# A scan beside attention: its pairs' ranks set 80 apart instead of 50

## The chip, the cores and the metric

The kernel runs on one core of a Trainium2 chip. A core has five engines that each run their own queue of instructions in order: TensorE (PE; matrix products, its weight loads are counted apart as PEld), VectorE (DVE), ScalarE (ACT), GpSimd (POOL) and SyncE (SP, which here only issues transfers). The time is device microseconds of one execution. Before the change, three runs gave a median of 3282.74 us (3273.26 to 3292.82).

## The reference

The kernel computes one block of a transformer over 1024 tokens (a grid of 16 by 64) and 256 context tokens, width 1024. A modulated layer norm is projected to three kinds of columns. Those of the first kind go to a neighbourhood attention with 8 heads of 64, those of the second to a two-directional RWKV scan with 8 heads of 64, those of the third are gates. The two results are merged and go through a router to a mixture of 16 experts.

```
row_block(i):                       # attention: one row of the grid
    kb, vb = window of 8 rows x 16 columns around each query
    s = [qi.kb * scale + bias, qi.k_ctx * scale];  p = softmax(s)
    return p_loc.vb + p_ctx.v_ctx
...
scan, per direction and head:       # state S (64 x 64), token by token
    S = decay(w) * S + rank-one updates from (kk, a) and (k, v);  y = r.S
...
y = group_norm(y_forward + y_backward) + bonus * v;  y = y * g      # readout
merged = gate_a * (na.w_pa) + gate_b * (y.w_pr);  x += merged.w_o
router -> top tokens per expert -> gated MLP of width 2816 -> x
```

## The kernel before, in words

Products of full precision are split into a high and a low part, so that one product becomes two or three on PE.

The stages are written one after another, but they are not run so. A scheduler takes the instructions of all engines and writes each engine's queue: of what is ready it puts the one with the lowest priority number first. The number counts up as instructions are written, and a `with low_priority(tc,n)` adds n to it for what is written inside. Each engine then runs its queue in order and waits at each instruction for what it needs.

- *Projection* (L264, `pp`) with the features of the scan and a small inversion (L298 to L326). It fills the transfers that the scan later loads.
- *Scan*, `rwkv_chain`. There are 20 pairs (j, n), and a pair is two steps, one for each direction d. A step loads five operands on SP (cAV, cX, cWT, cBT, cAU, L550 to L554, double-buffered), makes eight groups of eight 64x64 products (L541, through `mm`), reads `RU` on ACT into R (L559) and U (L566), and updates the state S on DVE (L568, L569). The trace has two records for each product, so a pair leaves 256 records of L541. The next step of the same direction needs S.
- *Attention*, `attention`, in two halves. The first takes head pairs 0 and 1, the second head pairs 2 and 3. For every head pair `run` first prepares Q and K: loads qz on ACT's queue (L633), a shuffle on DVE (L635), the rotation on POOL (L636 to L638), then KH, KL and Q (L642, L643, L648, L649). Then follow eight blocks. A block has scores `sc` and `sl` (L594 to L597), the bias and row maximum on DVE (L598, L599; each leaves two records per head, so four of L598 a block), the exponential on ACT (L602), scaling on DVE (L605), transposes `apt` (L612) and copies `pT` (L614, L616), and the products with V (L619).
- *Readout* (L677 to L702): eight tiles that add both directions' y, normalise and transpose them. L702 is a tile's last instruction. Readout and the second half of the attention need PSUM that the scan holds, so they begin when it ends.
- *Modulation* (L119, L120) for the merge.
- *Branches*: the attention result times w_pa and the scan's times w_pr, L716, 384 products; the one with w_pr comes first. Its weights are loaded by SP into `mwr` (L708), in memory that the fourth head pair's preparation frees (`done` in `run`). Then L759 merges, and the router and the experts follow.

The second head pair of each half follows the first as its blocks run out, so a preparation stands between the blocks of two head pairs.

Of the kernel before, what the change touches and what calls it, by code (L numbers as in the profile page):

```python
# [151 lines left out]
def mixer(octx, tc, i, G, keep, mc, dbg=None):  # L152
# [32 lines left out]
    with ExitStack() as c1:  # L185
# [300 lines left out]
        with ExitStack() as cw:  # L486
            wk=pool(cw,"wk",2,side="right"); pR=pool(cw,"wkR",1,space=PS,side="right")
            rwkv_chain(wk,pR,tc,i,G)
# [30 lines left out]
def tblock(j,d):  # L519

    return 0 if j==0 else (j if d==0 else 5-j)

def rwkv_chain(p,pR,tc,i,G):


    nc=tc.nc; vD=G["vD"]; yD=G["yD"]
    S=[p.tile([128,4,64],F32,name=f"S{d}",bufs=1) for d in range(2)]
    DL=[p.tile([128,4,20],F32,name=f"DLs{d}",bufs=1) for d in range(2)]
    for d in range(2): nc.sync.dma_start(DL[d],G["DLD"][d].rearrange("a p c -> p a c"))
    H=[slice(0,64),slice(64,128)]  # L530
    VS={}
    for b in (0,1,4,2,3):
        VS[b]=p.tile([128,4,4,64],F32,name=f"V{b}",bufs=1)
        for h,hh in zip(H,range(2)):
            nc.sync.dma_start(VS[b][h],vD[b*256:b*256+256,hh].rearrange("(c p) a f -> p c a f",p=64))
    def mm(o,l,r,first=None,stop=False):

        for ct in range(4):
            for hh,h in enumerate(H):
                b=first is not None and len(first)<2  # L540
                z=nc.tensor.matmul(o[h,ct],l[h,ct],r[h,ct],start=b,stop=stop,skip_group_check=True)  # L541
                if b: first.append(z)
                elif first: tc.add_manual_dep(z.ins,first[hh].ins.name,mybir.DependencyInfo(mybir.DependencyClass.NoSync,mybir.DependencyReason.DATA),reason="order")
    def step(j,n,d):
        main=j>0; tb=tblock(j,d); c=n if d==0 else 3-n; cc=tb*4+c
        first=(j==0 and n==0); M=128 if main else 64
        X,AV=[p.tile([128,4,128],F32,name=f"{z}{d}") for z in ("cX","cAV")]
        AU,WT,U=[p.tile([128,4,64],F32,name=f"{z}{d}") for z in ("cAU","cWT","U")]; V=VS[tb][:,c]
        BT=p.tile([128,2,4,64],F32,name=f"cBT{d}")
        nc.sync.dma_start(AV[:,:,:M],G["AVD"][d][cc][:,:,:M])  # L550
        nc.sync.dma_start(X[:,:,:M],G["XD"][d][cc][:,:,:M])
        nc.sync.dma_start(WT,G["WD"][d][cc].rearrange("h s a t -> (h s) a t"))
        nc.sync.dma_start(BT,G["BTD"][d][cc])
        if main: nc.sync.dma_start(AU,G["AUD"][d][cc])  # L554
        RU=pR.tile([128,2,4,64],F32,name=f"RU{d}"); YS=pR.tile([128,2,4,64],F32,name=f"YS{d}")
        mm(RU[:,0],AV[:,:,0:64],V,[],first)
        if not first: mm(RU[:,0],X[:,:,0:64],S[d],stop=True)
        R=p.tile([128,4,64],F32,name=f"R{d}",bufs=1)
        nc.scalar.activation(R,RU[:,0],AF.Copy,scale=-1.0)  # L559
        f=[]  # L560
        mm(YS[:,1],BT[:,1],V,f)
        if main:
            mm(YS[:,0],AV[:,:,64:128],V,f)
            mm(YS[:,0],X[:,:,64:128],S[d])
        mm(RU[:,1],WT,R,stop=True)
        nc.scalar.copy(U,RU[:,1])  # L566
        mm(YS[:,1],BT[:,0],U,stop=True)
        if not first: nc.vector.tensor_add(S[d],S[d],YS[:,1])  # L568
        nc.vector.tensor_tensor(S[d],YS[:,1] if first else S[d],DL[d][:,:,cc:cc+1].to_broadcast([128,4,64]),op=ALU.mult)  # L569
        if main:  # L570
            mm(YS[:,0],AU,U,stop=True)
            Y=p.tile([128,4,64],F32,name="Y",bufs=3)
            nc.scalar.copy(Y,YS[:,0])
            for h,hh in zip(H,range(2)): nc.sync.dma_start(yD[d][(cc-4)*64:(cc-3)*64,hh],Y[h])
    for j in range(5):
        for n in range(4):
            with low_priority(tc,2920-96*(4*j+n)):
                for d in range(2): step(j,n,d)

def attention(p,pr,tc,i,G):  # L580
# [527 lines left out]
```

## Time and profile before

| what | value |
|---|---|
| median of 3 runs | 3282.74 us |
| profiled execution | 3280.36 us |
| its span | 3278.5 us |
| mean granted TensorE clock | 0.947 |
| PE busy | 3018.6 us (92%) |
| DVE busy | 2291.9 us (70%) |
| ACT busy | 1732.9 us (53%) |
| POOL busy | 592.8 us (18%) |

The profile is of one execution. Busy time is the time in which an engine runs an instruction; PE's products are pipelined, so a busy PE is not PE at its peak. The granted clock is what the chip's throttle allowed, 1.00 being 2.4 GHz. The scan, the first half of the attention, the readouts and the start of the second half lie between about 890 and 1393 us of the span; the experts take the second half of it.

### The profile page before, as it was taken

Reading aid. Unit: us, or ns where it says so; the run is one execution under the profiler, and the core shown is the slowest. Engines: PE = TensorE matmul, PEld = TensorE weight load, DVE = VectorE, ACT = ScalarE, POOL = GpSimd, SP = SyncE. Lnnn points to the kernel's source line nnn. Section 1 sums busy time; section 2 is a strip of 40 time slices with the busy share of each in tenths; the row PEclk is TensorE's granted clock in tenths of the full one; section 3 lists DMA queues with packets and bytes.
Section 4 is the critical chain, followed back from the end, with each engine's and each line's share of the span. In section 5 each row is a group of like instructions: output and inputs, shape, how many; then the busy total and the mean of one; then the engine's idle time right before and its main releaser. Section 6 shows DMA issues by size and latency. Waiting matters only on the chain.

```text
span 3278.5 us, 51242 instructions
## 1 busy us (share of the span) xinstructions
PE 3018.6 (92%) x19868; PEld 2390.2 (73%) x19868; DVE 2291.9 (70%) x3049; ACT 1732.9 (53%) x2006; POOL 592.8 (18%) x429
## 2 busy tenths in 40 slices
PE   7998999997779988799979999999999999999996
PEld 4777777775568763477748888788888888888884
DVE  5246356454233448757878988888988889889887
ACT  5343433333122333432337777777777777777775
POOL 2243333333030027303000000110001111000004
PEclk8999989997789999799979999999999999999998
DMA  5345554554757546345389999999999999999985
GB/s 202 80 124 134 136 129 106 136 149 111 188 164 213 160 146 209 95 128 175 138 314 372 370 368 371 359 379 382 364 365 357 359 373 374 377 366 357 365 320 223
DMA packets 559510, 822.80 MB, mean 251 GB/s; under 512 B 233182, under 2 KB 360798, under 8 KB 559140
## 3 DMA queue, kind: packets, MB, share of 16 engines
q1 hardware_dynamic: 515292, 749.19, 66.2%
q10 hardware_dynamic: 38616, 50.82, 4.6%
q0 software_dynamic: 5360, 19.54, 2.3%
q8 instruction: 156, 2.56, 0.3%
q14 instruction: 86, 0.70, 0.1%
HBM read 729.86 MB, written 89.55 MB: 250 GB/s over the span
## 4 chain that ended last, share of the span: by engine, by line
PE 43%; DVE 6%; issue 3%; DMA 2%; ACT 2%; POOL 1%; ACTq 0%; POOLq 0%; DVEq 0%
PE ph L1023 21%; PE ye L1038 14%; DVE lo L922 4%; PE pA L716 3%; PE po L759 2%; DMA raw<-in_w_e_dram 1%; PE pt L1060 1%; ACT hi L921 1%; DVE oh L863 0%; DVE dl L1062 0%; PE pl L835 0%; PE yp L619 0%; ACT xh L893 0%; PE apt L612 0%; DMA acc<-yo,idx 0%
## 5 line engine op out<-in xcount | busy, mean ns | idle before, releaser
L922 DVE TENSOR_TENSOR lo<-raw,hi 128x2048 fp32r<-128x2048 f32 (+1 forms) x560 | 1197.2, 2169 | 110.7 <-ACT hi L921 94.6
L921 ACT CAST hi<-raw 128x2048 fp32r<-128x2048 f32 (+1 forms) x560 | 1010.0, 1814 | 355.9 <-PE ph L1023 193.8
L1023 PE MATMUL ph<-lo,xh 128*128 128x512 f32 (+1 forms) x1536 | 457.5, 379 | 23.3 <-DVE lo L922 22.9
L1023 PE MATMUL ph<-hi,xh 128*128 128x512 f32 (+1 forms) x1536 | 449.7, 375 | 3.1 <-ACT xh L893 2.0
L1023 PE MATMUL ph<-hi,xl 128*128 128x512 f32 (+1 forms) x1536 | 449.3, 374 | 0.0
L1023 PEld LDWEIGHTS ph<-lo,xh 128*128 128x128 f32 x1536 | 268.1, 189 | 95.5 <-DVE lo L922 48.3
L1023 PEld LDWEIGHTS ph<-hi,xh 128*128 128x128 f32 x1536 | 272.3, 189 | 56.2 <-ACT xh L893 2.4
L1023 PEld LDWEIGHTS ph<-hi,xl 128*128 128x128 f32 x1536 | 271.6, 189 | 52.7
L264 PE MATMUL pp<-uh,whi 128*128 128x512 f32 (+1 forms) x832 | 268.4, 393 | 14.7 <-ACT gate L271 3.9
L264 PE MATMUL pp<-ul,whi 128*128 128x512 f32 (+1 forms) x832 | 269.0, 392 | 0.0
L264 PE MATMUL pp<-uh,wlo 128*128 128x512 f32 (+1 forms) x832 | 265.4, 389 | 0.2 <-POOL wlo L213 0.2
L1038 PE MATMUL ye<-lo,dh 128*128 128x512 f32 x704 | 222.5, 397 | 1.2 <-DVE lo L922 1.2
L1038 PE MATMUL ye<-hi,dh 128*128 128x512 f32 x704 | 219.6, 393 | 2.5 <-ACT hi L921 1.3
L1038 PE MATMUL ye<-hi,dl 128*128 128x512 f32 x704 | 218.9, 392 | 3.3 <-DVE dl L1062 3.3
L871 POOL DMA_INDIRECT gath<-table,idx x16 | 37.8, 2363 | 962.0 <-DVE oh L863 587.7
L264 PEld LDWEIGHTS pp<-uh,whi 128*128 128x128 f32 x832 | 155.3, 196 | 52.7 <-issue 7.1
L264 PEld LDWEIGHTS pp<-ul,whi 128*128 128x128 f32 x832 | 156.0, 195 | 40.8 <-issue 12.5
L264 PEld LDWEIGHTS pp<-uh,wlo 128*128 128x128 f32 x832 | 156.5, 196 | 35.5 <-issue 5.0
L213 POOL TENSOR_TENSOR wlo<-wraw,whi 128x512 fp32r<-128x512 f32 x86 | 112.3, 1323 | 263.2 <-ACT whi L212 227.3
L1038 PEld LDWEIGHTS ye<-hi,dl 128*128 128x128 f32 x704 | 132.8, 189 | 32.1 <-DVE dl L1062 3.7
L298 DVE TENSOR_TENSOR tmp<-AU,W 120x144 f32<-120x144 f32 (+24 forms) x248 | 96.9, 391 | 84.5 <-DMA AU<-aD 38.6
L1038 PEld LDWEIGHTS ye<-hi,dh 128*128 128x128 f32 x704 | 131.1, 189 | 30.7 <-ACT hi L921 2.0
(334 smaller groups left out, 4552.0 us busy)
## 6 DMA issues: line engine op xcount, KB each, us to landing
raw<-in_w_e_dram SPq DMA_DIRECT2D x430, 1024.0 KB
raw<-in_w_e_dram SPq DMA_DIRECT2D x128, 768.0 KB
wraw<-in_w_in_dram SPq DMA_DIRECT2D x86, 256.0 KB
wmod<-in_w_mod_dram SPq DMA_DIRECT2D x48, 256.0 KB
BTD<-BT SPq DMA_DIRECT2D x160, 64.0 KB
cBT<-BTD SPq DMA_DIRECT2D x40, 256.0 KB
wmod<-in_w_mod_dram SPq DMA_DIRECT2D x16, 512.0 KB
XD<-X SPq DMA_DIRECT2D x32, 256.0 KB
```

The costliest lines, as they stand in the source:

```text
L213: nc.gpsimd.tensor_sub(l[:,ks],r,h[:,ks].bitcast(F32))
L264: nc.tensor.matmul(p,wt[:,k,:],ut[:,k,a:a+b],start=(k==0 and first),stop=(k==7 and last))
L298: nc.vector.tensor_tensor(v,AU[d][:,:,s,ts_][:,:,None,:].to_broadcast([120,2,nj,L]), W[d][:,:,js,s:s+1].to_broadcast([120,2,nj,L]),op=ALU. ...
L716: nc.tensor.matmul(pq[q],w[:,kk,:],y[:,kk,q*512:(q+1)*512],start=(kk==0 and first),stop=(kk==3 and last))
L759: nc.tensor.matmul(pq[q],a[:,r],w[:,q*512:(q+1)*512],start=(k==0 and first),stop=(k==7 and last))
L871: gi=nc.gpsimd.indirect_dma_start(out=g,out_offset=None,in_=table[:,:], in_offset=bass.IndirectOffsetOnAxis(ap=idx[:,:1],axis=0))
L921: nc.scalar.copy(hi[:,:2*w],r[:,:2*w])
L922: li=nc.vector.tensor_sub(lo[:,:2*w],r[:,:2*w],hi[:,:2*w].bitcast(F32))
L1023: nc.tensor.matmul(PH[m][j][:,:c.stop-c.start],x[:,k,:],y[:,c],start=(k==0 and a),stop=(k==7 and b))
L1038: nc.tensor.matmul(ye[j],l[:,k,:],rr[:,j*512:(j+1)*512],start=st and a,stop=sp and b)
L1060: for k in range(n): nc.tensor.transpose(pt[:,k,:],hd[:,(k0+k)*128:(k0+k+1)*128],ident)
```

## The change

One number: the priority that is added to a pair of steps. A pair's two steps count the priority up by 146. Taking away 96 from pair to pair leaves the ranks 50 apart, and 66 leaves them 80 apart; the first pair's rank stays, and the last pair's becomes 570 larger.

```diff
     for j in range(5):
         for n in range(4):
-            with low_priority(tc,2920-96*(4*j+n)):
+            with low_priority(tc,2920-66*(4*j+n)):
                 for d in range(2): step(j,n,d)
```

The scheduler writes other queues from this. The first block of the attention stood behind 465 of the scan's 2352 products on PE and now stands behind 626; all 16 blocks of the first half stand before the scan's end now, where 12.5 did. Three places show it.

The first is PE at the end of the scan (`RU` and `YS` are scan results, `sc`, `sl`, `apt` and `yp` belong to attention; the two name numbers of a tile tell copies apart). Before:

```order
L619 MATMUL yp<-pT,vc 64x128 x4
L612 MATMUL apt<-ident,s 120x128 x4
L594 MATMUL sc<-KH_11751,Q_11749 128x256
L595 MATMUL sc<-KL_11753,Q_11749 128x256
L541 MATMUL YS_10596<-U_10588,cBT_10589 64x64 x8
L596 MATMUL sl<-KH_11751,Q_11749 128x320
L597 MATMUL sl<-KL_11753,Q_11749 128x320
L619 MATMUL yp<-pT,vb 64x128 x4
L612 MATMUL apt<-ident,s 120x128 x2
L612 MATMUL apt<-ident,s 80x128 x2
L541 MATMUL YS_10596<-U_10588,cAU_10586 64x64 x8
L594 MATMUL sc<-KH_11752,Q_11750 128x256
```

After:

```order
L541 MATMUL YS_10424<-U_10416,cAU_10414 64x64 x8
L541 MATMUL RU_10595<-S_7460,cX_10584 64x64 x7
L541 MATMUL YS_10510<-U_10502,cAU_10500 64x64 x8
L541 MATMUL RU_10595<-S_7460,cX_10584 64x64
L541 MATMUL YS_10596<-V_7468,cBT_10589 64x64 x8
L541 MATMUL YS_10596<-V_7468,cAV_10585 64x64 x8
L541 MATMUL YS_10596<-S_7460,cX_10584 64x64 x8
L541 MATMUL RU_10595<-R_10613,cWT_10587 64x64 x8
L541 MATMUL YS_10596<-U_10588,cBT_10589 64x64 x8
L541 MATMUL YS_10596<-U_10588,cAU_10586 64x64 x8
L594 MATMUL sc<-KH_12642,Q_12640 128x256
L595 MATMUL sc<-KL_12644,Q_12640 128x256
```

The last products of the scan stood among blocks; now they stand together, and the next `sc` after them is the first of the second half (KH_12642).

The second is DVE near the last S updates (L568, L569), with the third head pair's preparation (`KL_12644`, `KL_12645`, `Q_12640`, `Q_12641`). After:

```order
L643 TENSOR_TENSOR KL_12645<-qz,KH_12643 64x256 x2
L614 COPY pT<-apt 128x512
L635 STREAM_SHUFFLE qy<-qz 128x512
L649 TENSOR_TENSOR Q_12640<-qz,Q_12640 64x2x128 x2
L649 TENSOR_TENSOR Q_12641<-qz,Q_12641 64x2x128 x2
L635 STREAM_SHUFFLE qy<-qz 128x512
L649 TENSOR_TENSOR Q_12640<-qz,Q_12640 64x2x128 x2
L649 TENSOR_TENSOR Q_12641<-qz,Q_12641 64x2x128 x2
L635 STREAM_SHUFFLE qy<-qz 128x512
L623 TENSOR_TENSOR yl_11147<-yp,yh_11146 128x4x32
L568 TENSOR_TENSOR S_7460<-S_7460,YS_10080 128x256
L569 TENSOR_TENSOR S_7460<-S_7460,DLs_7462 128x256
```

These rows of the preparation stood behind the last S update and among readouts before:

```order
L603 RECIPROCAL m<-m 128x2
L605 TENSOR_SCALAR s<-s,m 128x696 x2
L700 TENSOR_TENSOR z<-pA,gsb 128x512
L688 TENSOR_REDUCE gs<-y_12386 128x8
L643 TENSOR_TENSOR KL_12644<-qz,KH_12642 64x512 x2
L598 ISA s,m<-sc,zero 128x256
L598 ISA m 128x1
L689 TENSOR_SCALAR gs<-gs 128x8
L643 TENSOR_TENSOR KL_12644<-qz,KH_12642 64x512 x2
L599 ISA s,m<-sl,bt,m 128x320
L599 ISA m 128x1
L702 TENSOR_TENSOR yl_11149<-z,yh_11148 128x4x128
```

The preparation moved from the readouts into the scan.

The third is DVE at the end of the readouts, with the fourth head pair's preparation (`KL_13230`, `KL_13231`) and the 8th L702. Before:

```order
L603 RECIPROCAL m<-m 128x2
L702 TENSOR_TENSOR yl_11149<-z,yh_11148 128x4x128
L600 TENSOR_SCALAR m<-m 128x2
L623 TENSOR_TENSOR yl_11147<-yp,yh_11146 128x4x32
L605 TENSOR_SCALAR s<-s,m 128x696 x2
L791 CAST tok<-affV 128x16
L614 COPY pT<-apt 128x512
L603 RECIPROCAL m<-m 128x2
L605 TENSOR_SCALAR s<-s,m 128x696 x2
L643 TENSOR_TENSOR KL_13230<-qz,KH_13228 64x512 x2
L598 ISA s,m<-sc,zero 128x256
L598 ISA m 128x1
```

After:

```order
L643 TENSOR_TENSOR KL_13230<-qz,KH_13228 64x512 x4
L700 TENSOR_TENSOR z<-pA,gsb 128x512
L598 ISA s,m<-sc,zero 128x256
L598 ISA m 128x1
L688 TENSOR_REDUCE gs<-y_12566 128x8
L643 TENSOR_TENSOR KL_13231<-qz,KH_13229 64x512 x4
L614 COPY pT<-apt 128x512
L623 TENSOR_TENSOR yl_11147<-yp,yh_11146 128x4x32
```

Here four of the eight L702 are still to come. The last of them stands behind the first L710, the split of the weights for the branch:

```order
L700 TENSOR_TENSOR z<-pA,gsb 128x512
L598 ISA s,m<-sc,zero 128x256
L598 ISA m 128x1
L710 TENSOR_TENSOR mwl<-mwr,mwh 128x512
L599 ISA s,m<-sl,bt,m 128x440
L599 ISA m 128x1
L702 TENSOR_TENSOR yl_11149<-z,yh_11148 128x4x128
```

The fourth head pair's rows stood behind the 8th L702 and now stand among the last readouts, and the first L710 with its load no longer comes after the preparation that followed them. From the scan's end to the first branch product 14 blocks and two preparations stood on PE and DVE, now 10 blocks and one preparation. From the first L759 to the end, PE's, ACT's and POOL's queues are the same.

## Rows read from the trace of the kernel before

**Rows 1.** Windows, all engines: us, busy PE, PEld, DVE, ACT, POOL, PEclk, DMA, GB/s.
```profile
1207.30:1349.00 141.70, 119.10 (x654) 61.60 (x650) 111.55 (x247) 56.50 (x130) 86.26 (x62) 0.92 0.60 187
1349.00:1392.60 43.60, 25.55 (x128) 17.50 (x127) 31.39 (x73) 19.56 (x46) 9.56 (x11) 0.57 0.28 86
1392.60:1516.30 123.70, 120.94 (x691) 96.02 (x690) 74.38 (x149) 39.71 (x81) 19.51 (x7) 0.99 0.43 132
...
1080.00:1200.00 120.00, 110.45 (x1845) 86.34 (x1843) 51.99 (x141) 40.30 (x104) 15.41 (x12) 0.94 0.46 133
```

**Rows 2.** Windows of line L541 alone: us, PE busy, PEld busy, PEclk, DMA, GB/s.
```profile
1000.00:1060.00 60.00, 46.41 (x1391) 43.31 (x1389) 1.00 0.73 221
1060.00:1132.80 72.80, 48.40 (x1040) 39.35 (x1035) 1.00 0.55 163
1132.80:1160.40 27.60, 15.38 (x278) 12.56 (x273) 0.75 0.54 160
1160.40:1207.30 46.90, 27.96 (x650) 23.17 (x650) 1.00 0.36 101
```

**Rows 3.** Windows of line L598 alone: us, DVE busy, PEclk, DMA, GB/s.
```profile
1000.00:1060.00 60.00, 1.71 (x8) 1.00 0.73 221
1060.00:1132.80 72.80, 3.43 (x16) 1.00 0.55 163
1132.80:1160.40 27.60, 0.00 (x0) 0.75 0.54 160
1160.40:1207.30 46.90, 3.43 (x16) 1.00 0.36 101
```

**Rows 4.** DVE by shape, 1207.3 to 1349.0: xcount | busy us, mean ns | idle.
```profile
L605 DVE TENSOR_SCALAR s<-s,m 128x576 f32<-128x576 f32 x12 | 10.7, 933 | 0.1
L598 DVE CUSTOM_DVE_ANT_0 s<-sc,zero 128x256 f32<-128x256 f32 x22 | 9.2, 418 | 3.9 <-PE sc L595 2.4 <-PE apt L612 1.5
...
L643 DVE TENSOR_TENSOR KL<-qz,KH 64x512 fp32r<-64x512 f32 x8 | 8.1, 1009 | 0.1
L599 DVE CUSTOM_DVE_ANT_0 s<-sl,bt,m 128x440 f32<-128x440 f32 x12 | 8.1, 672 | 2.9 <-DMA bt<-in_bias_dram 2.8
...
L649 DVE TENSOR_TENSOR Q<-qz,Q 64x256 fp32r<-64x256 f32 x8 | 7.5, 971 | 1.6 <-ACT Q L648 1.5
...
L614 DVE COPY pT<-apt 128x512 f32<-128x512 f32 x10 | 6.8, 681 | 0.0
L605 DVE TENSOR_SCALAR s<-s,m 128x696 f32<-128x696 f32 x8 | 6.2, 821 | 0.1
...
L599 DVE CUSTOM_DVE_ANT_0 s<-sl,bt,m 128x320 f32<-128x320 f32 x10 | 5.5, 548 | 1.2 <-DMA bt<-in_bias_dram 1.0
...
L635 DVE STREAM_SHUFFLE qy<-qz 128x512 f32<-128x512 f32 x4 | 2.9, 727 | 0.0
```

**Rows 5.** Timeline of PE: start us, us, engine, line, operation, xcount.
```profile
928.38 0.63 PE L541 MATMUL RU<-S,cX 64*64 64x64 f32 x16
928.85 0.63 PE L541 MATMUL YS<-V,cBT 64*64 64x64 f32 x16
...
1126.29 0.33 PE L541 MATMUL YS<-V,cAV 64*64 64x64 f32 x2
1126.55 0.33 PE L612 MATMUL apt<-ident,s 128*120 128x128 f32 x1
1126.80 0.32 PE L541 MATMUL YS<-V,cAV 64*64 64x64 f32 x2
```

**Rows 6.** Timeline, single instructions of DVE, SP's queue and PE.
```profile
1206.87 0.42 DVE L569 TENSOR_TENSOR S<-S,DLs 128x256 f32<-128x256 f32 x1
...
1348.54 0.67 DVE L702 TENSOR_TENSOR yl<-z,yh 128x512 fp32r<-128x512 f32 x1
...
1380.52 0.38 SPq L708 DMA_DIRECT2D mwr<-in_w_pr_dram  x1
...
1392.64 1.05 PE L716 MATMUL pA<-yh,mwh 128*128 128x512 f32 x2
```

## The prediction

> **What bounds the kernel now.** I read the windows of the stages first, then the DVE groups by shape inside them, then single rows of the timeline. The kernel is one long chain on TensorE (PE): it is busy 92% of the span, and the rank edit leaves everything from the first L759 to the end in the same order on PE, ACT and POOL. So only the stretch from the scan's start near 890 us to the first L759 at 1516.3 us can change, some 626 us of the 3280.4 us of the profiled execution. This execution lies 2.4 us under the median of the runs shown; I form the sum against its own time and add the 2.4 us at the end.
>
> That stretch has three parts whose ends the landmarks give [rows 6]: the scan, until the last S update at 1206.87 us; a part with readouts, attention and modulation, until the first branch product at 1392.64 us (185.4 us); and the branch part, 123.7 us, until L759. In the branch part PE is busy 120.94 of 123.70 us at clock 0.99: PE bounds it. In 1207.3 to 1349.0, PE is busy 119.10 and DVE 111.55 of 141.70 us: neither leaves much. In 1349.0 to 1392.6 nothing is full (PE 25.55 of 43.60 at clock 0.57, DVE 31.39): here the kernel waits, and the lower granted clock follows the idle engine [rows 1]. What ends this lull is a chain: the 8th readout ends at 1348.5 us, then the fourth head pair's Q and K are prepared, their pool is closed, only then does the w_pr load start (1380.52 us), and 12 us later the branch runs [rows 6].
>
> In the scan part the amount of scan work per microsecond tells the price of what is put beside it [rows 2, 3]. A pair leaves 256 records of L541, a block of attention 4 records of L598. 1000 to 1060 us holds 5.43 pairs and 2 blocks, 1060 to 1132.8 us 4.06 pairs and 4 blocks, 1160.4 to 1207.3 us 2.54 pairs and 4 blocks. The rate where products stand packed (16 records in 0.47 us [rows 5]) makes a bare pair 256/16 x 0.47 = 7.5 us. With that the three stretches without a preparation give (60 - 40.7)/2 = 9.6, (72.8 - 30.4)/4 = 10.6 and (46.9 - 19.0)/4 = 7.0 us per block; solving the first against the second gives a pair 6.9 and a block 11.2, the first against the third 8.8 and 6.1. I take 8.7 us, the middle, and keep 6.1 and 11.2.
>
> **The change part by part.** Nothing is added or removed; 40 steps get new places. The moves are counted in the orders of before and after, of which the section on the change shows three places.
>
> *Three and a half more blocks inside the scan.* Before, 12.5 of the first half's 16 blocks stand on PE ahead of the scan's end, now all 16, in pairs 8 to 17, and the last three pairs have no attention beside them. 3.5 blocks x 8.7 = 30 us, and I add 27 more changes between scan products and others, of which PE's rows show the price: two scan records and one L612 between them repeat every 0.51 us where packed ones need 2 x 0.029 + about 0.3, so 0.15 us per change [rows 5], 4 to 5 us in all. Term 1: +35 us, bounds 3.5 x 6.1 = 21 and 3.5 x 11.2 + 5 = 44.
>
> *The third head pair's preparation inside the scan.* Its L643 and L649 rows now stand between S updates of pairs 16 and 17; before, they stood after the last update. The second head pair's preparation shows the price: 1132.8 to 1160.4 us has 1.09 pairs (8.2 us at 7.5) and no block, 19.4 us more than the pair needs, at clock 0.75 [rows 2, 3]. That is an upper bound, since no work but the preparation and the pair stands there. The DVE rows of one preparation are 8.1 (L643) + 7.5 (L649) + 2.9 (L635) = 18.5 us in the three large groups [rows 4]; DVE is busy only 51.99 of 120 us from 1080 to 1200 us [rows 1], so pairs can run beside a good part of them. Term 2: +10 us, the middle between 0 (the pairs pass it) and 19. The S updates behind these rows on DVE are waited for by PE, R and U on ACT, so here a stall is a stall of the scan.
>
> *The first scan product 20 projection rows later.* The same rows of L264 run ahead of it instead of beside it: 0, since PE does both either way.
>
> *What is left between the scan's end and the branch.* Before 14 blocks, 2 preparations, 8 readouts and the modulation; now 10 blocks and one preparation, and this one stands on DVE beside the last four readouts; the first L710, which splits the w_pr weights, even stands three rows ahead of the 8th L702, so that the branch can run as soon as the 8th readout is done. From the PE side: the 141.7 us to the 8th readout hold 11 blocks, as the L598 rows show (22 scores), and 10 are left, so they lose one block at the 8.7 us of term 1; and 3 us come on for the w_pr load (before, 12 us from its issue to the first L716 [rows 6]), in case it is late, most of which blocks can fill: 136 us. From the DVE side: 111.55 + 31.39 = 143 us of work, less 4 blocks at (10.7 + 9.2 + 8.1 + 6.8 + 6.2 + 5.5)/11 = 4.2 us [rows 4] and one preparation at 18.5, leaves 107.5 us; at the share of 111.55/141.70 = 79% that is 136 us. Both give 136 us. Term 3: 136 - 185.4 = -49 us; bounds -78 (DVE full, 107.5 us) and -35 (the lull shrinks, but a preparation still queues behind readouts, 150 us).
>
> *The branch part.* One block fewer lies beside L716, and PE is full there: -5 us, bounds 0 and -7. The work after L759 doesn't move: 0.
>
> Sum: +35 + 10 - 49 - 5 = -9 us, so 3271.4 us against the profiled execution, and 3274 us with the 2.4 us.
>
> **Two rules weighed.** PE is busy 110.45 of 120 us between 1080 and 1200 us, weight loads 86.34 [rows 1]. The Trainium skill, "Perfetto Trace Analysis", Identifying the Most-Contended Engine, holds matmul busy time to be a poor measure, since matmuls are pipelined, and wants the busy share of the weight loads instead. By it PE has 28% of room in the scan and added blocks should slip in at the low end, which is rival B; the three prices above, 7.0 to 10.6 us per block, don't bear it out fully.
>
> A scan product is a 64x64 tile, an attention product takes 128 rows. The Trainium skill, "TensorEngine Tiling (Array Packing)", Key Properties, says that changing the tiling mode drains TensorE, and so speaks against interleaving. The 0.15 us per change agrees with some such cost; with about 330 changes in all and 27 more, it is 4 us by the row, and it would support rival C if the drain grew with the density of changes.
>
> **The rivals.**
> *A, the forecast:* the lull goes, the scan pays most of it back. Net -26 to +2, 3257 to 3285 us, by the 6.1 to 11.2 us per block alone.
> *B, blocks slip in:* the added blocks cost 6.1 us each and the preparation hides wholly beside the scan products: +21 + 0 - 49 - 5 = -33, 3250 us. For it: DVE is busy only 51.99 of 120 us from 1080 us, so blocks and preparation find room there. Against: PE is busy 110.45 of the same 120 [rows 1].
> *C, slower:* ten pairs now carry 1.6 blocks each, a density that before stood only in the last 46.9 us (1.57; it was 1.0 from 1060 to 1132.8 us). If the price there is 11.2 us and the preparation stalls the S updates for 19, the scan is 44 + 19 = 63 us longer, while the part behind gives 35 only: +28, 3311 us. It decides once a block costs over 11 us beside the scan with a stalled preparation. For it: 10.6 us at 1.0 blocks per pair; the last three pairs, alone, can be held by their own round of PE, ACT and DVE instead of filling it with attention. Against: 7.0 us at 1.57 blocks per pair.
> *D, the change does nothing that counts:* the readouts are paced by their own chain of loads, POOL and DVE (POOL 86.26 of 141.70 us busy [rows 1]) and end 142 us after the scan as before, so what the scan loses is what the lull gives: +45 - 43.6 - 5 = -4, 3279 us. Against: one block and a preparation fewer stand among them on DVE.
>
> **How the numbers follow.** A 0.45, B 0.15, C 0.28, D 0.12. What a measurement of this kernel can tell from no change is 0.5%, 16.4 us: faster means below 3266, slower above 3299. A lies to 0.20 in faster, 0.24 in same, 0.01 in slower; B 0.15 in faster; C 0.05 in same and 0.23 in slower; D 0.11 in same and 0.01 in slower. That makes 0.35, 0.40 and 0.25. The range reaches 12 us below B, towards term 3's bound of -78, and up to C: 3238 to 3312 us; A alone is 3257 to 3285.
>
> **What would show it.** Right: the last S update some 45 us later, near 1252 us; no lull before the first L716, which runs about 136 us after the last S update, near 1388; from L716 to L759 some 119 us. The granted clock stays at 2.4 GHz (1.00) through the last three pairs. Wrong in term 1 or 2: the scan's end at over 1270 us, with DVE rows L643 between S updates and PE waiting for L568. Wrong in term 3: the 8th L702 still over 140 us after the last S update, or w_pr's load still more than 20 us behind it. Wrong altogether: a difference after L759.

## The result, and the profile after

Eight runs of the changed kernel gave a median of 3262.32 us (3254.69 to 3264.76), eight of the kernel before beside them 3277.36 us. The ratio of the means is 0.9941, interval [0.9926, 0.9956]: faster by 0.6%; the medians differ by 15 us, 0.5%. The forecast was 3274 us against 3282.74 us, a ratio of 0.997: the right way, and about half of the size.

The profiled execution took 3259.49 us, with a span of 3257.7 us at clock 0.950. The landmarks of the kernel after, which answer to [rows 6] (start us, us, engine, line):

```profile
1241.98 0.42 DVE L569 TENSOR_TENSOR S<-S,DLs 128x256 f32<-128x256 f32 x1
...
1370.66 0.69 DVE L702 TENSOR_TENSOR yl<-z,yh 128x512 fp32r<-128x512 f32 x1
...
1363.33 0.38 SPq L708 DMA_DIRECT2D mwr<-in_w_pr_dram  x1
...
1378.16 0.63 PE L716 MATMUL pA<-yh,mwh 128*128 128x512 f32 x2
```

The w_pr load is now issued before the 8th readout ends, and the first L716 runs 7 us behind that readout instead of 43. The windows of the same stages, as in [rows 1] (us, then busy PE, PEld, DVE, ACT, POOL, clock, DMA share, GB/s):

```profile
1242.40:1371.40 129.00, 109.62 (x568) 54.64 (x564) 105.00 (x227) 51.59 (x116) 77.64 (x56) 0.91 0.65 204
1371.40:1378.20 6.80, 5.77 (x46) 3.78 (x46) 4.64 (x16) 3.45 (x8) 1.01 (x5) 1.00 0.34 102
1378.20:1495.10 116.90, 114.86 (x648) 91.65 (x647) 69.09 (x136) 37.46 (x73) 19.61 (x7) 1.00 0.43 136
...
1495.10:3257.00 1761.90, 1674.77 (x8084) 1365.34 (x8084) 1536.37 (x1378) 1196.42 (x978) 159.45 (x86) 0.98 0.91 342
```

The stretch of 43.6 us at clock 0.57 is gone. From the first L759 on, both kernels take the same time to half a microsecond (1762.6 us to the end of the span here, 1762.2 us before). The same window before:

```profile
1516.30:3278.00 1761.70, 1676.32 (x8084) 1367.66 (x8084) 1535.84 (x1378) 1196.60 (x978) 158.36 (x86) 0.98 0.91 342
```

So the whole difference lies where the prediction put it. The last S update ends at 1242.4 us (35.1 later), the stretch from there to L716 takes 135.8 us (49.6 less), the branch part 116.9 us (6.8 less): 35.1 - 49.6 - 6.8 = -21.3 us. That is the difference of two executions, the one of before 3 us above its kernel's median and the one of after 3 us below; the medians differ by 15 us.

In the scan the L541 rows, as in [rows 2] (us, PE busy, PEld busy, clock, DMA share, GB/s), show where it pays:

```profile
953.60:971.50 17.90, 10.80 (x267) 10.18 (x267) 0.77 0.75 240
1104.00:1190.00 86.00, 48.31 (x1067) 39.92 (x1066) 0.98 0.53 156
1192.80:1221.80 29.00, 13.15 (x265) 12.08 (x263) 0.66 0.37 109
1221.80:1242.40 20.60, 18.39 (x605) 17.99 (x603) 1.00 0.47 131
```

The third line is the third head pair's preparation: 29.0 us for 1.04 pairs, at clock 0.66. The last is the pairs that run alone: 605/256 = 2.36 pairs in 20.6 us, 8.7 us each. What the scan waits for in the third line is seen on ACT, whose queue holds the preparation and the scan's copy U (L566) in one order:

```profile
1200.01 0.41 ACT L648 CAST Q<-qz 64x256 fp32r<-64x256 f32 x1 [4.93 <-POOL qz L638]
...
1200.32 1.13 ACT L648 CAST Q<-qz 64x256 fp32r<-64x256 f32 x3
...
1205.84 0.33 ACTq L633 DMA_DIRECT2D qz<-kD  x1
...
1206.82 1.44 ACT L648 CAST Q<-qz 64x256 fp32r<-64x256 f32 x4
...
1214.06 0.33 ACTq L633 DMA_DIRECT2D qz<-kD  x1
...
1217.88 0.37 ACT L566 COPY U<-RU 128x256 f32<-128x256 f32 x1 [2.03 <-DMA vb<-vnD]
```

A chunk of Q goes from a load to DVE, POOL, ACT and back to DVE, and the next load waits until DVE has read the chunk, some 8 us a round (1205.84 to 1214.06). The two loads shown, `qz<-kD`, already fetch K for the fourth head pair, most of whose preparation comes behind the scan. U stands behind these rounds, and S and the next R behind U.

### The profile page after: what moved, and what is told of

The parts are those of the page before. It is cut to its first block, busy times and chain, and to the rows that moved or that the text cites. A ratio compares the mean times of both kernels' runs of the same rounds, so it can differ in the third digit from the quotient of the medians.

```text
span 3257.7 us, 51229 instructions
## 1 busy us (share of the span) xinstructions
PE 3013.3 (92%) x19868; PEld 2382.1 (73%) x19868; DVE 2299.9 (71%) x3049; ACT 1733.9 (53%) x2006; POOL 591.6 (18%) x429
## 4 chain that ended last, share of the span: by engine, by line
PE 48%; DVE 9%; DMA 3%; issue 3%; ACT 2%; POOL 1%; ACTq 0%; SPq 0%; POOLq 0%; DVEq 0%
PE ph L1023 22%; PE ye L1038 14%; DVE lo L922 4%; PE pA L716 3%; PE po L759 2%; PE YS L541 1%; PE pt L1060 1%; DMA raw<-in_w_e_dram 1%; ACT hi L921 1%; PE yp L619 1%; PE apt L612 1%; PE RU L541 1%; DVE dl L1062 1%; DVE oh L863 0%; DVE KL L643 0%
```

## The experiments

All times in this table are from the profiled executions; ratios are to the kernel before on the same chip. "Scan" runs from the first L541 on PE to the end of the last S update, "behind" from there to the first L716, "branch" on to the first L759. "Changes" counts, in PE's queue from the first to the last product of the scan, how often a scan product follows another product or the other way round. The profile is of one execution, up to 10 us off its kernel's median (in e10 and e12 10 us above it, in e6 7 us below), so differences of a few microseconds in these columns mean little: e7 and the changed kernel, with 326 changes and 16 blocks in the scan both, differ by 4 us there.

| kernel | ratio, interval | scan | behind | branch | changes | blocks in the scan |
|---|---|---|---|---|---|---|
| before | 1 | 315.5 | 185.4 | 123.7 | 298 | 12.5 |
| changed | 0.9941 [0.9926, 0.9956] | 344.2 | 135.8 | 116.9 | 326 | 16 |
| e1 late readouts | 0.9999 [0.9984, 1.0015] | 316.4 | 182.2 | 123.9 | 298 | 12.5 |
| e2 four qz, changed | 1.0054 [1.0037, 1.0071] | 376.4 | 137.3 | 113.4 | 334 | 16 |
| e3 four qz, before | 1.0085 [1.0068, 1.0101] | 340.4 | 189.5 | 114.8 | 312 | 12.5 |
| e4 12 blocks, changed | one run, 3263.6 us | 340.9 | 143.7 | 117.2 | 278 | 12 |
| e5 new, then old ranks | 1.0037 [1.0024, 1.0049] | 375.1 | 139.8 | 115.5 | 410 | 16 |
| e6 old, then new ranks | 1.0030 [1.0015, 1.0044] | 363.2 | 146.5 | 119.4 | 332 | 16 |
| e7 more DVE, changed | one run, 3270.6 us | 348.4 | 147.6 | 112.2 | 326 | 16 |
| e8 rotation on DVE, changed | 1.0000 [0.9986, 1.0015] | 363.2 | 134.9 | 116.9 | 342 | 16 |
| e9 40 apart | 0.9920 [0.9900, 0.9940] | 293.5 | 182.1 | 125.1 | 104 | 12 |
| e10 110 apart | 0.9841 [0.9825, 0.9858] | 315.9 | 134.7 | 118.3 | 216 | 16 |
| e12 110 apart, 200 lower | 1.0019 [1.0004, 1.0033] | 371.4 | 140.4 | 117.0 | 372 | 16 |

**e1, the lull filled without touching the scan.**

```diff
-        readout(ro,rps,tc,i,G,yh1,yl1)
+        with low_priority(tc,2500): readout(ro,rps,tc,i,G,yh1,yl1)
```

> The kernel before with its scan ranks, but the eight readouts rank 2500 later: the scan's queue is the same, and the last readouts stand beside the fourth head pair's preparation, with the same 14 blocks and two preparations between the scan's end and the first branch product. Theory L (the gain of the change is the lull that goes, because readouts now stand beside that preparation): the stretch from the last S update to the first L716 shrinks from 185 to 155-170 us, ratio to before 0.990 to 0.996. Theory W (the stretch is paced by the amount of DVE work in it, about 143 us at 77%, and the gain is that work leaves it for the scan): 180-190 us, ratio 0.998 to 1.002.

The 8th L702 moved from 1349.2 to 1378.8 us, beside the fourth preparation, and the lull between it and the first L716 shrank from 43 to 16 us. Nothing was gained: 182.2 us. Theory L falls. The windows of the stretch in the kernel before, in e1 and in the changed kernel:

```profile
1207.30:1392.60 185.30, 144.65 (x780) 79.10 (x777) 142.94 (x319) 76.06 (x176) 95.82 (x73) 0.83 0.53 163
```
```profile
1213.00:1395.20 182.20, 140.80 (x775) 76.57 (x774) 140.06 (x313) 75.69 (x175) 94.41 (x73) 0.85 0.54 166
```
```profile
1242.40:1378.20 135.80, 115.39 (x613) 58.42 (x610) 109.64 (x242) 55.03 (x124) 78.66 (x61) 0.91 0.63 199
```

DVE is busy 77%, 77% and 81% of it, PE 78%, 77% and 85%: the length goes with the work in the stretch, wherever the lull lies. By these three lines alone that could be DVE's work or PE's.

**e7, more work for DVE there.**

```diff
         nc.vector.tensor_sub(yl[:,:,r],z,yh[:,:,r].bitcast(F32))
+        for _ in range(4): nc.vector.tensor_copy(y2,y)
```

> The changed kernel with four more copies of 128x512 on DVE behind each of the eight readouts, 32 x 0.68 = 22 us of DVE work that nobody needs. Theory W (the stretch from the last S update to the first L716 is paced by its DVE work, 110 of 136 us): it lengthens by 20-28 us to 156-164 us and the kernel by as much. If PE or the readouts' chain paces it: 0-8 us more.

```profile
L703 DVE COPY y<-y 128x512 f32<-128x512 f32 x30 | 18.3, 608 | 0.2
...
1248.40:1396.00 147.60, 120.93 (x657) 63.42 (x653) 119.43 (x286) 59.94 (x134) 75.43 (x56) 0.91 0.59 189
```

Thirty of the 32 copies lie in this stretch and took 18.3 us. DVE's busy time there rose by only 9.8 us (119.43 against 109.64): one L702 moved behind the first L716, one block more came in, and most of the rest is that the same rows took less time than in the changed kernel (the 16 of L686 and L691 together 2.6 us less, the 12 of L643 1.7 us less). The stretch is 11.8 us longer, less than theory W's 20 to 28 us and more than its rival's 0 to 8 us. DVE's share stayed at 81% while PE's fell from 85% to 82%, which speaks for DVE; over the thirteen kernels of the table DVE's share of this stretch lies between 77% and 83%, PE's between 77% and 87%. It is one run, and that DVE alone sets the pace is not shown. Which work counts is plainer: where the third head pair's preparation stands inside the scan, the stretch takes 135 to 148 us, and where it stands behind (before, e1, e3, e9), 182 to 190 us.

**e2 and e3, four buffers for the chunks of Q and K.**

```diff
-                    z=pr.tile([128,512],F32,name="qz"); ...
+                    z=pr.tile([128,512],F32,name="qz",bufs=4); ...
```

> The changed kernel with four buffers of qz instead of two. Theory Q (the 29 us stretch at the third head pair's preparation inside the scan is ACT's queue waiting at the qz load for a free buffer, with the scan's U copy queued behind it): that stretch falls to 10-16 us, the last S update comes at 1215-1230 instead of 1242 us, ratio to before 0.985 to 0.990. Theory P (the price is the preparation's own DVE and ACT work in front of the S updates): last S update at 1236-1244, ratio 0.992 to 0.996.

> The kernel before with four buffers of qz and the old ranks. Theory Q: the second preparation's stretch in the scan (27.6 us for 1.09 pairs) falls to 12-18, and the fourth preparation, one after another behind the 8th readout, shortens by 5-10 us of the lull: ratio to before 0.993 to 0.997. Theory P: 0.998 to 1.002.

Both theories missed, Q by its sign: the scan became 32 and 25 us longer. With more buffers the scheduler set preparations closer together (in e2 all 20 rows of L643 and L649 of the second one stand between two S updates, at 1088.9 and 1119.9 us), and the first two preparations of e2 hold a pair for 38 us each. More buffers did not make a preparation cheap for the scan.

**e8, the rotation on DVE.**

```diff
-                        nc.gpsimd.tensor_mul(z,z,rope[:,0,cs])
+                        re=nc.vector if ct<3 else nc.gpsimd; re.tensor_mul(z,z,rope[:,0,cs])
...
```

> The changed kernel with the rotation of Q and K (three products and sums a chunk, 4.1 us on POOL) on DVE for the three preparations inside the scan. Theory R (a preparation costs the scan its round trips: load, shuffle on DVE, POOL, ACT, DVE, one chunk after another, with the scan's R, U and S queued between them): each preparation is 5-10 us cheaper, the stretch of the third falls from 29 to 17-24 us, last S update at 1222-1234, ratio to before 0.986 to 0.992. Theory P (the price is the DVE and ACT rows themselves): 10 us more DVE work per preparation, last S update at 1242-1255, ratio 0.994 to 0.999.

The last S update came at 1257.9 us and the ratio at 1.0000, both a little beyond what theory P said. At the third preparation a pair took 24 us instead of 30, as theory R said of that one, but at the second it took 35 instead of 28, and the scan as a whole became 19 us longer. The gain that theory R forecast did not come.

**e4, four blocks left out.**

```diff
-                    block(ps,B,ct,ii,hc,Q2,KH,KL,vc,vb,bt)
+                    if B==1 and ii==3:
+                        for z in (yh,yl): nc.gpsimd.memset(...,0.0)
+                    else: block(ps,B,ct,ii,hc,Q2,KH,KL,vc,vb,bt)
```

> The changed kernel with 4 of the first half's 16 blocks left out (the last four rows of the grid of head pairs 0 and 1 are zero instead). It gives the price of a block beside the scan. At the 8.7 us of the prediction the last S update comes 35 us earlier than 1242, at 1207; at the lower bound of 6.1, 24 us earlier, 1218; at 11.2, 45 us earlier, 1197. If the last pairs are limited by something else, it hardly moves: over 1230.

The last S update came at 1238.7 us, 3.7 us earlier: none of the three prices, and over the 1230 us that were to tell of another limit. It is not the last pairs that were the limit, since the last five take 5 to 10 us each; the pairs that have blocks beside them take 22 to 30 us each, where the changed kernel's take 17 to 30 us. So a block has no constant price beside the scan. The scheduler wrote another order here too, so what replaces the price this run does not tell.

**e5 and e6, half of the ranks changed.**

```diff
-            with low_priority(tc,2920-96*(4*j+n)):
+            with low_priority(tc,2920-66*min(4*j+n,10)-96*max(4*j+n-10,0)):   # e5
+            with low_priority(tc,2920-96*min(4*j+n,10)-66*max(4*j+n-10,0)):   # e6
```

> Ranks 80 apart for the first ten pairs, 50 apart for the last ten. All 16 blocks and the third head pair's preparation still stand inside the scan, the preparation at its very end. Theory M (the gain is 3.5 blocks and a preparation that left the DVE-paced stretch behind the scan, less what they cost in the scan): last S update at 1235-1250, 130-142 us from there to L716, ratio to before 0.991 to 0.997. Theory S (the gain is made at the start, where two more pairs run beside the last projections): the same ratio, so this run alone doesn't tell them apart.

> Ranks 50 apart for the first ten pairs, 80 apart for the last ten. The scan's start stands as before, and all 16 blocks and the third preparation stand inside the scan, that one at S updates 38 and 39. Theory M: the gain of the change less the 9 us that the start gave: last S update at 1248-1258, 130-140 us from there to L716, ratio to before 0.994 to 0.999. Theory S: no gain, 0.999 to 1.004.

Both are slower than before. e5 missed the ratio that both theories gave it, so the new ranks at the start alone do not bring the gain, as theory S had it. e6's ratio of 1.0030 is the one of theory S, and M's is missed, though the last S update at 1252.7 us is where M put it. In both the stretch behind the scan is short (139.8 and 146.5 us; M gave 130 to 142 and 130 to 140). But both scans cost more than the changed kernel's, by 31 and 19 us, and that outweighs it. e5 equals the changed kernel up to the tenth pair; then each pair carries about one block and takes 20 us (pairs 13 to 18 end at 1118, 1140, 1160, 1179, 1199 and 1219 us). The changed kernel has 1067/256 = 4.17 pairs in the 86 us from 1104 to 1190 us, 20.6 us a pair, and seven blocks start there, 1.7 a pair. PE is not idle in e5's stretch, it is busy 96.33 of the 101 us. Its rows show what it does (start us, us):

```profile
1136.34 0.32 PE L612 MATMUL apt<-ident,s 128*120 128x128 f32 x1
1136.59 0.27 PE L541 MATMUL YS<-U,cBT 64*64 64x64 f32 x1
1136.60 0.27 PE L541 MATMUL YS<-S,cX 64*64 64x64 f32 x1
1136.70 0.22 PE L541 MATMUL YS<-U,cBT 64*64 64x64 f32 x1
1136.71 0.22 PE L541 MATMUL YS<-S,cX 64*64 64x64 f32 x1
1136.86 0.33 PE L612 MATMUL apt<-ident,s 128*120 128x128 f32 x1
```

One transpose, four records of the scan, one transpose: PE's queue changes between the two kinds 410 times instead of 326. A fit over eight stretches of five kernels (time = a x pairs + b x other products + c x changes) gave 7.5, 0.106 and 0.21 us, three constants from eight points. From here on this was theory C.

**e11, a change measured by itself.**

```diff
+    def grouped():
+        for g in range(4):
+            for k in range(32): small(k)      # a product of 64x64
+            for k in range(16): turn(k)       # a transpose of 128x128
+    def mixed():
+        for k in range(64):
+            small(0); small(1)
+            turn(k)
```

> The kernel before with a probe behind the last expert, where nothing else runs: twice a grouped stretch (four times 32 products of 64x64, then 16 transposes of 128x128) and a mixed one (64 times two products of 64x64 and one transpose). Both hold 128 products and 64 transposes; a mixed one has 120 changes more. Theory C: a mixed stretch takes 120 x 0.21 = 25 us more (by the 0.15 us that the prediction read from one row, 18 us). If a change costs nothing and the price lies in queues and waits: 0-4 us more.

The mixed stretch and the grouped one behind it, both at full clock and with PE busy throughout:

```profile
3289.83:3323.11 33.28, 33.28 (x321) 21.23 (x320) 0.00 (x0) 0.00 (x0) 0.00 (x0) 1.00 0.01 1
3323.11:3338.75 15.64, 15.64 (x321) 14.70 (x321) 0.00 (x0) 0.00 (x0) 0.00 (x0) 1.00 0.01 2
...
3325.13 1.97 PE L1078 MATMUL pt<-ident,yo 128*128 128x128 f32 x16
3327.02 2.08 PE L1077 MATMUL pt<-yo 64*64 64x64 f32 x64
```

The same products take 17.6 us more, so 17.6/120 = 0.147 us a change. That is less than the fit's 0.21. It is the 0.15 us that the prediction read from [rows 5], but by luck: the reading took 0.3 us for a packed transpose, which takes 0.118 us here (16 from 3325.13 to 3327.02), and counted one change in a period that holds two. With both put right the same row gives (0.51 - 0.058 - 0.118)/2 = 0.17 us. The probe has transposes only; the scan's products also change with those of `sc`, `sl` and `yp`, whose price was not measured.

**e9, e10 and e12, other ranks, chosen by their changes.**

```diff
-            with low_priority(tc,2920-96*(4*j+n)):
+            with low_priority(tc,2920-106*(4*j+n)):   # e9
+            with low_priority(tc,2920-36*(4*j+n)):    # e10
+            with low_priority(tc,2720-36*(4*j+n)):    # e12
```

> Ranks 40 apart (step 106). On PE 12 of the 16 blocks stand inside the scan and the third preparation behind it, as before, but PE's queue changes 104 times between scan products and others instead of 298 (changed kernel: 326). Theory C (what is put beside the scan costs 0.21 us for each change between scan products and others on PE, 0.106 us for each other product, on 7.5 us for a pair, as a fit over eight stretches of five kernels gives): the scan from its first product to the last S update takes 275-290 instead of 315 us, ratio to before 0.988 to 0.994. Theory B (a block beside the scan is cheap only where two of them run at once and dear, 12 us, where one runs per pair, however they are cut): 310-325 us, ratio 0.998 to 1.004.

> Ranks 110 apart (step 36). All 16 blocks in pairs 2 to 13, two and more per pair, the third preparation between S updates 25 and 28, the last six pairs alone, 216 changes on PE instead of 326. Theory C: the scan takes 344 - 110 x 0.21 = 321 us and the part behind it 130-140 us as in the changed kernel, ratio to before 0.984 to 0.991. Theory B: two blocks per pair as in the changed kernel, 338-350 us, ratio 0.992 to 0.998.

> Ranks 110 apart as in the fastest run so far, but all 200 lower (2720-36k). All 16 blocks in pairs 6 to 13, two and more per pair, the third preparation between S updates 27 and 30, the last five pairs alone; PE changes 372 times instead of 216. Theory C: the scan takes 316 + 156 x 0.21 = 349 us, some 10 us of which an earlier start gives back, ratio to before 0.989 to 0.997. Theory B (two or more blocks at once are what makes them cheap): as that run, 0.981 to 0.987.

e9 and e10 came as theory C said and not as B, in e9 3.5 us above C's scan of 275 to 290: with closer ranks than before and 104 changes the scan is 22 us shorter, and with 216 changes the scan that holds all 16 blocks and the third preparation takes as long as the one before that held 12.5 blocks and no third preparation. e10 is the fastest of all, 3231.42 us (ratio 0.9841 to before; its profiled execution, 3241.18 us, was the slowest of its four). e12 has the spacing of e10 and blocks as dense, but 372 changes, and its scan is 55 us longer. This is 22 us beyond what C said (349 us), and not at all what B said of it, so B falls. PE's busy time in the scans of e10 and e12:

```profile
911.20:1227.10 315.90, 275.53 (x5389) 230.37 (x5390) 155.15 (x390) 115.76 (x294) 54.36 (x42) 0.90 0.58 173
```
```profile
900.70:1272.10 371.40, 320.34 (x5435) 253.26 (x5436) 162.97 (x390) 118.14 (x297) 56.71 (x43) 0.89 0.51 149
```

Of the 55.5 us, 44.8 are PE's busy time for the same kind of work, and the rest is idle time. The 156 changes at the probe's price make 23 us. Another part is the granted clock: in e12's scan 66.8 us of PE's busy time lie at the lower level of 1.2 GHz, in e10's 48.5 us. The longest such stretch of e12, behind its first preparation, and sixteen records of the scan in it:

```profile
993.70:1027.90 34.20, 26.67 (x227) 19.25 (x226) 19.21 (x43) 9.14 (x21) 10.07 (x8) 0.50 0.28 79
...
1005.15 1.12 PE L541 MATMUL YS<-U,cAU 64*64 64x64 f32 x16 [2.48 <-DVE S L568]
```

Sixteen such records take 0.63 us in [rows 5], at clock 1.00, and 1.12 us here, so the 18.3 us more at the lower clock are some 8 us of loss, an estimate. That leaves some 14 us of PE's busy time unexplained.

In the same way 84 changes make 12 of the 31 us between e5 and the changed kernel, and 110 make 16 of the 28 us between the changed kernel and e10. Between e9 and the kernel before, 194 changes make 29 us and the scan is only 22 us shorter. So the price of a change is shown by the probe. Among the kernels with one step for all pairs and like work in the scan, the scan is longer the more changes there are (104 and 298; 216, 326 and 372). But the count alone does not tell a scan's length: e2, e6 and e8 have 332 to 342 changes and scans 19 to 32 us longer than the changed kernel with 326, and e4 has 48 changes and four blocks less than that and is 3 us shorter. What else goes with it (PE's busy time beyond the probe's price and the clock, preparations that hold a pair for 27 to 38 us) stays open.

## Why the prediction was right, point by point

- *Where it can change:* right. The time behind the first L759 differs by less than half a microsecond.
- *The stretch behind the scan, -49 us:* measured -49.6. Of its two workings the one by DVE's work holds (107.5 us forecast, 109.64 measured, at 81% instead of 79%). The one by the lull gave the same number by luck: e1 filled most of the lull and gained 3 us. DVE was in fact busy 31.39 of the 43.60 us of the lull, 72%, nearly its share of the stretch before it. The gain comes from work that left a stretch in which DVE is busy 77% of the time for one in which it is busy 115 of 315 us; that DVE paces the former is supported by e7, not proven. The count of blocks in the working was off: the queue has 11.5 blocks behind the scan now, not 10, which the blocks' smaller DVE rows, left out of the 4.2 us, made up for in part.
- *The branch part, -5 us:* measured -6.8, within its bounds.
- *What the scan pays, +45 us:* measured +35.1. This is the size that was off, and its parts were off in both directions, so that part of the nearness is luck. The preparation's stretch is 29.0 us for 1.04 pairs, so 21 us and not 10: beyond the bound of 19. The start was costed at 0 and gave some 9 us: when the first preparation's hold of a pair ended, at 971.5 us, six pairs had ended, where before four had at 964.6, and 2 pairs at 8 us less the 7 us are 9. That leaves 35 + 9 - 21 = 23 us for 3.5 blocks, 6.6 each, where I took 8.7 and the changes. The sum had no term for the clock in the scan: PE's busy time at 1.2 GHz there rose from 34.8 to 50.6 us, by the rows of e12 some 7 us of loss (an estimate), which lies inside these prices.
- *A price per block:* the step that does not carry. That it gave a fair number here is luck: e5, e6 and e12 have the same blocks and the same preparation inside the scan and pay 19 to 31 us more, e6 with hardly more changes (332 against 326); e4 has four blocks fewer and pays nearly as much.
- *Rival C:* its sign was wrong for this change. One half of its condition held, since the preparation stalls the scan for 21 us where it said 19; the other did not, since the blocks came to 6.6 us each and not 11.2. Density as such does not decide: e10 holds up to 2.5 blocks in a pair and is the fastest. The price of a change on PE, weighed beside this rival, is part of what separates these kernels. The Trainium skill, "TensorEngine Tiling (Array Packing)", Key Properties, says that a change of the tiling mode drains TensorE; the probe shows a price for such a change, 0.147 us, and not whether it is a drain.
- *Rival D:* the readouts did not keep their pace: the 8th ended 129 us behind the scan, not 142.
- *Rival B:* not borne out: the preparation did not hide.
- *The bounds and chances:* with 6.1 to 11.2 us a block the terms of rival A add up to -23 to 0, not -26 to +2. By the prediction's own limit of 3266 us the result of 3262 us counts as faster, to which it gave 0.35, less than the 0.40 for the same.

## What to carry to other kernels

Where an engine is nearly full in one stretch and has room in its neighbour, work can gain by moving between them, and filling a lull inside such a stretch brought next to nothing here (e1): weigh the busy time of the fullest engines over the whole stretch before putting a price on a wait. When small products are laid between large ones, count how often PE's queue changes between the two kinds, since this can be read from the order alone: at 0.147 us each, the 156 changes between e10 and e12 make 23 of 55 us. It is no full account, as e2, e4, e6 and e8 show. A rank step is no smooth knob: between 40, 80 and 110 apart, with half-way mixes and another base, the ratio to before went from 0.984 to 1.004, so several values are worth a run.

## What was not expected of the hardware

A change on PE between 64x64 products and 128x128 transposes costs 0.147 us at full clock, more than the transpose itself when grouped (16 in 1.9 us, 0.118 us each); in the profile it hides as busy time, since PE was busy 33.28 of 33.28 us in the mixed stretch. More buffers for a loaded operand made the kernel before slower by 0.8% (e3); the queues' order changed with them, and that this is the reason is not shown.
